# Attention in one fixed TensorE order over all 32 units, with 14 dense tiles woven in

## The chip, the cores and the metric

The kernel runs on one core of a Trainium2 chip. The metric is the device time of one execution in microseconds (us), the median of several runs. TensorE (PE; its weight loads are PEld) multiplies matrices and writes into PSUM, eight banks of 128 x 512 floats. VectorE (DVE), ScalarE (ACT) and GpSimd (POOL) work element by element; SyncE (SP) issues the transfers. Each engine has one queue of its own and works it in order; semaphores hold an instruction until what it needs is there.

## The reference

One layer of a streaming encoder: 1024 positions, width 1024. Attention picks 256 keys per query by an indexer's scores; beside it stands a Mamba-2 mixer (SSD); both are gated and merged; a SwiGLU follows. Cut to what the change touches:

```python
h = rmsnorm(x, pre_norm_mix) * (1.0 + scale_m) + shift_m
proj = h @ w_in          # columns: q_lat, kv_lat, k_idx, w_idx, z, xbc, dt, g_a, g_b
# A: attention, 16 heads of 128 latent columns, blocks of 128 queries
q = (rmsnorm(q_lat, q_norm) @ w_uq).reshape(B, L, 16, 128)
kv = rmsnorm(kv_lat, kv_norm)
_, idx = lax.top_k(iscore, 256)          # indexer scores, causal by chunks of 64
logits = einsum('bqhc,bqkc->bhqk', q_b, kv[idx]) * scale + rel_bias[bucket]
probs = softmax(where(valid, logits, -inf))
o = einsum('blhc,hcd->blhd', einsum('bhqk,bqkc->bqhc', probs, kv[idx]), w_uv)
# B: SSD
xbc = silu(causal_depthwise_conv(xbc, conv_w) + conv_b)   # 32 tiles of 128 channels
y = ssd(xbc, dt, a_log)
y = rmsnorm(y * silu(z), ssd_norm)                        # z: 16 tiles
mix = (sigmoid(g_a) * (o @ w_o_attn) + sigmoid(g_b) * (y @ w_o_ssd)) @ w_out   # g_a, g_b: 8 tiles each
```

## The kernel before, in words

Everything lies transposed: channels on the 128 partitions, positions along the row, in two halves of 512. Floats are split into a high and a low part, and a product is made of three (high x high, high x low, low x high). A dense tile of `w_in` (128 output channels, both halves) is therefore 48 TensorE products of 128 x 512; its sums stand in the tiles called `pw`. Weights come through a stream (`W`, lines 133 to 161): SP loads 128 x 512 floats, ScalarE copies the high part (line 151), GpSimd makes the low part (line 152), with three buffers of each.

Attention does not gather. Top-k (lines 616 to 716, VectorE and ScalarE) ends in a mask `MK` per block of queries (line 702); masked scores are computed for all keys. A **unit** is (hp, u): two heads, 256 queries (two blocks, t = 0 and 1), and so `2u + 2` blocks of 128 keys. There are 8 x 4 = 32 units, u in the order 0, 2, 1, 3. Each unit has two generators, which hand over control at every `yield`:

- `att_scores` (line 730): the query products `puq` (12 products), the copies `qh` on ScalarE (737) and `ql` on VectorE (738), and then, in four steps (t and head hh), the score products `plg` (766), VectorE's masked minimum out of PSUM (775) and ScalarE's Exp into `lg` (778).
- `att_out` (line 783): for each block j of keys a `turn`: two or four transposes of `lg` into a bank `pt` (799), and one copy `pc` out of it, on VectorE for odd j (802) and on ScalarE for even j (804). After all turns the products with the values `vt` (815), which use half of the array's columns and add up in the bank `po`, and the scaling and store (818 to 820).

`attention` (line 848) runs the scores of one unit beside the output of the unit before it through `weave`, which only sets the order of the program. The compiler's scheduler then orders each engine's queue anew, by a simulated timeline, with program order as priority: an instruction that is ready may pass one that is not. `in_order(...)` (line 108) ties the instructions of the named engines to program order; here `ATT_ORDER` is empty, so attention is not tied.

The order of the program is: indexer, top-k; attention of hp 0 to 2 (line 881); the dense tiles of `FILL` (line 936): five groups of four convolution tiles (`x`), 16 tiles of z, 8 of g_a, and three more convolution groups (`X`), 56 tiles in all; attention of hp 3 to 7 (line 947); SSD with the tiles of g_b and the attention projection beside it; merge; SwiGLU. A convolution tile ends in ScalarE's scaled copy (911), nine VectorE instructions (914 to 916) and Silu (921); for `X` two tiles share one chain of four Silu.

PSUM is split into two pools: three banks `bank_d` (dense tiles, and `pt` for hp 3 and above), five banks `bank` (`puq`, `plg`, `po`, and `pt` for hp below 3). `vt`, the values of two heads, has one buffer (855). After each unit `ada_next` (872) does a piece of the modulation vector (GpSimd, VectorE, two tiny products `adap`).

Of the kernel before, what the change touches and what calls it, by code (L numbers as in the profile page):

```python
# [17 lines left out]
P = 128  # L18
# [12 lines left out]
LOWEST = -BIGGEST  # L31
QC = 256
ORDERED = (mybir.EngineType.PE, mybir.EngineType.Activation, mybir.EngineType.DVE)
FILL = "xxxxx" + "z" * 16 + "a" * 8 + "XXX"
HP_FIRST = 3
LEAD = 1.5
U_ORDER = (0, 2, 1, 3)
ATT_ORDER = ()
NCH = L // QC
LAST = ((0, 0, 512), (1, 0, 256), (1, 256, 256))  # L40
FFN_GROUPS = [4, 4, 4, 4, 3, 3]
# [26 lines left out]
def build(tc, a, dbg=None, stop=99, slots=None):  # L68
# [26 lines left out]
    def half(b):  # L95
        return slice(512 * b, 512 * b + 512)
# [5 lines left out]
    def dump(key, ap, idx=None):  # L102
        if dbg is not None and key in dbg:
            d = dbg[key] if idx is None else dbg[key][idx]
            SP.dma_start(d, ap)
# [27 lines left out]
    class Stream:  # L133
# [21 lines left out]
        def next(self):  # L155
            self.used += 1
            while len(self.tiles) < min(self.used - 1 + self.ahead, len(self.q)):
                self.load()
            return self.tiles[self.used - 1]
# [11 lines left out]
    def col_tile(w):  # L171

        kt = w.shape[1]
        return [(w[:, k:k + min(4, kt - k)], min(4, kt - k)) for k in range(0, kt, 4)]
# [608 lines left out]
    def att_out(hp, u, vt, PR):  # L783

        r2 = sm.tile([P, 2, 2, 64], F32, name="r2", bufs=1)
        G.tensor_copy(r2, PR["rr"].rearrange("p (t h) -> p t h", t=2)[:, :, :, None].to_broadcast([P, 2, 2, 64]))
        po = bank("po")
        pov = po[:, 0:256].rearrange("p (t n) -> p t n", t=2)
        last = 2 * u + 1
        parts = {}  # L790

        def turn(j):
            ts = (0, 1) if j < last else (1,)
            sl = slice(ts[0], 2)
            pt = (bank if hp < HP_FIRST else bank_d)("pt")
            ptv = pt.rearrange("p (h t n) -> p h t n", h=2, t=2)
            for hh in range(2):
                for t in ts:
                    T.transpose(ptv[:, hh, t, :], PR[hh, t][:, j * P:(j + 1) * P], ident)  # L799
            pc = Q("pc").rearrange("p (h t n) -> p h t n", h=2, t=2)  # L800
            if j % 2:
                V.tensor_copy(pc[:, :, sl], ptv[:, :, sl])
            else:
                S.activation(pc[:, :, sl], ptv[:, :, sl], AF.Copy)
            parts[j] = pc, sl

        for j in range(last + 1):
            turn(j)
            yield
        for t in range(2):  # L810
            T.transpose(po[:, 256 + 128 * t:384 + 128 * t], r2[:, t].rearrange("p h n -> p (h n)"), ident)
        for j in range(last + 1):
            pc, sl = parts.pop(j)
            for hh in range(2):
                T.matmul(pov[64 * hh:64 * hh + 64, sl], vt[:, j, 64 * hh:64 * hh + 64], pc[:, hh, sl],
                         start=j == 0, stop=j == last, skip_group_check=True)
        rb = sm.tile([P, 256], F32, name="rb", bufs=1)
        S.activation(rb, po[:, 256:512], AF.Copy)
        V.tensor_tensor(rb, po[:, 0:256], rb, op=OP.mult)
        SP.dma_start(d_att[hp][:, 256 * u:256 * u + 256], rb)  # L820
        yield

    def weave(x, nx, y, ny, z=iter(()), nz=0, lead=1):

        i = j = k = 0
        while i < nx or j < ny:
            if j >= ny or (i < nx and i * ny <= j * nx * lead):
                next(x, None)
                i += 1
            else:  # L830
                next(y, None)
                j += 1
            while k < nz and k * (nx + ny) < nz * (i + j):
                next(z, None)
                k += 1
        for g in (x, y):
            for _ in g:
                pass
# [6 lines left out]

    att = {}

    def attention(steps, last, beside=lambda: None):

        for s_ in steps + [None] * last:  # L850
            nxt = iter(())
            if s_ is not None:
                hp, u = s_
                if u == U_ORDER[0]:
                    vt = vp.tile([P, NT, P], F32, name="vt", bufs=1)
                    SP.dma_start(vt, d_v[hp])
                    att["w"] = small_weights(a["w_uq"][hp]), vt, load_bias(hp)
                uq, vt, nb = att["w"]
                PR = {}
                nxt = att_scores(u, uq, nb, PR)  # L860
            prev = att.get("prev")
            if prev is None:
                weave(nxt, 5, iter(()), 0)
            else:
                weave(nxt, 5 if s_ else 0, att_out(*prev), 2 * prev[1] + 3, lead=LEAD)
            if s_ is not None:
                att["prev"] = (hp, u, vt, PR)
            beside()
# [3 lines left out]
    def ada_next():  # L872
# [3 lines left out]
            ada_col(*late.pop(0))  # L876
        if j is not None:
            late.append(ada_slow(j))

    if stop != 3:  # L880
        attention([(hp, u) for hp in range(HP_FIRST) for u in U_ORDER], 0, ada_next)
        if stop == 4:
            attention([(hp, u) for hp in range(HP_FIRST, 8) for u in U_ORDER], 1)
    if stop == 4:
        for k in range(KT):
            for b in BS:
                t = EV("attd")
                SP.dma_start(t, d_att[k][:, half(b)])
                dump("attn", t, (k, slice(None), half(b)))
        ctx.close()  # L890
        return


    def wide(c):
        W.plan(col_tile(a["w_in"][c]))
# [11 lines left out]
    def conv(ch, dst):  # L907
        p = wide(17 + ch)
        ts = [EV("cv") for b in BS]
        for b in BS:  # L910
            S.activation(ts[b], p[b], AF.Identity, bias=col("conv_b", ch), scale=col("cw3", ch))
        for s, nm_ in ((1, "cw2"), (2, "cw1"), (3, "cw0")):
            w = col(nm_, ch)
            V.scalar_tensor_tensor(ts[0][:, s:], p[0][:, :512 - s], w, ts[0][:, s:], op0=OP.mult, op1=OP.add)
            V.scalar_tensor_tensor(ts[1][:, :s], p[0][:, 512 - s:], w, ts[1][:, :s], op0=OP.mult, op1=OP.add)
            V.scalar_tensor_tensor(ts[1][:, s:], p[1][:, :512 - s], w, ts[1][:, s:], op0=OP.mult, op1=OP.add)
        return [(ts[b], dst[:, half(b)]) for b in BS]

    def conv_out(outs):
        for t, dst in outs:  # L920
            S.activation(t, t, AF.Silu)
            SP.dma_start(dst, t)

    def conv_group(g, n):

        tiles = ((16 + g, d_bc[g, 0]), (24 + g, d_bc[g, 1]), (2 * g, d_xs[2 * g]), (2 * g + 1, d_xs[2 * g + 1]))
        for i in range(0, 4, n):
            outs = [o for t in tiles[i:i + n] for o in conv(*t)]
            if n > 1:
                with in_order(mybir.EngineType.Activation):  # L930
                    conv_out(outs[::-1])
            else:
                conv_out(outs)

    n_x, n_z, n_a = iter(range(GROUPS)), iter(range(16)), iter(range(8))
    for kind in FILL:
        if kind in "xX":
            conv_group(next(n_x), 2 if kind == "X" else 1)
        elif kind == "z":
            t = next(n_z)  # L940
            gate(1 + t, d_z[t], AF.Silu)
        elif stop != 3:
            t = next(n_a)
            gate(49 + t, d_sga[t], AF.Copy)
    if stop != 3:
        with in_order(*ATT_ORDER):
            attention([(hp, u) for hp in range(HP_FIRST, 8) for u in U_ORDER], 1, ada_next)
    for _ in range(35):
        ada_next()

# [111 lines left out]
    def beside():  # L1062

        for t in range(8):
            W.plan(col_tile(a["w_in"][57 + t]))
            w = wpieces(ks8)
            for b in BS:
                p = bank_d("pw")
                yield from dense_steps(p, b, w, Hs)
                o = EV("g")  # L1070
                S.activation(o, p, AF.Copy)
                SP.dma_start(d_gb[t][:, half(b)], o)
                yield
        AT = [([None, None], [None, None]) for _ in range(KT)]
        for b in BS:
            for k in range(KT):
                t = EV("atl")
                SP.dma_start(t, d_att[k][:, half(b)])
                AT[k][0][b], AT[k][1][b] = split(H_, t, "at", lo_eng=G if k % 2 else V)
        for t in range(8):  # L1080
            W.plan(col_tile(a["w_o_attn"][t]))
            w = wpieces(ks8)
            for b in BS:
                ya = EV("ya")
                p = bank_d("poa")
                yield from dense_steps(p, b, w, AT)
                V.tensor_copy(ya, p)
                SP.dma_start(d_ya[t][:, half(b)], ya)
                yield
# [431 lines left out]
```

## Time and profile before

| | us |
|---|---|
| median of 3 runs | 2464.05 |
| the runs | 2463.94, 2464.05, 2467.35 |
| span of the profiled execution, first to last instruction | 2459.8 |
| median less span | 4.25 |
| TensorE busy in the span | 2383.1 |
| last attention output, its copy (line 819) | 1148.9 |

The profiled execution's own device time is not listed; its span is, and the 4.25 us lie around it. In the profile a row of a group gives line, engine, operation, output and inputs, shapes and count, then the busy time and the mean in ns, then the idle time of the engine ahead of them and what ended it. A matmul's row is longer than the time it keeps the array, because matmuls overlap: starts have to be compared, not lengths. A transpose is one record; a product of plain floats is two.

### The profile page before, as it was taken

What the parts mean: (1) busy time and instruction counts of PE and PEld (TensorE: products, weight loads), DVE (VectorE), ACT (ScalarE), POOL (GpSimd) and SP (SyncE); (2) the same over time, 40 slices, a digit from 0 to 9 for tenths busy, and PEclk for the clock granted to TensorE, in tenths of its full rate; (3) what the DMA queues carried; (4) which work ended last, traced back from release to release, by engine and by line L of the source; (5) the groups of instructions that cost most, each with busy time, mean ns of one, the idle gap of its engine ahead of it and who ended that gap; (6) DMA issues with size and microseconds to landing.
All of it is one profiled execution on the core that took longest, in us unless ns stands there. A gap on an engine that the chain in (4) does not pass through costs nothing. (4 is left out here: it accounts for less than half of the span.)

```text
span 2459.8 us, 34881 instructions
## 1 busy us (share of the span) xinstructions
PE 2383.1 (97%) x11946; PEld 1931.1 (79%) x11946; DVE 1496.3 (61%) x3050; ACT 1183.7 (48%) x2285; POOL 1022.3 (42%) x829
## 2 busy tenths in 40 slices
PE   7999999999999999999999999999999999999996
PEld 5788888888788887777776767888777888888886
DVE  4566775698745556765558666455476666552336
ACT  4446665567445545556566565544454222352211
POOL 2722112222234334553336335656676555432233
PEclk9999999999999999999999999999999999999998
DMA  7224122523212222223768775654465444253132
GB/s 268 99 77 130 65 73 78 155 87 103 86 67 92 102 99 91 93 84 123 223 215 260 228 246 172 231 186 161 168 208 171 160 145 163 99 190 113 48 99 90
DMA packets 212834, 341.25 MB, mean 139 GB/s; under 512 B 21249, under 2 KB 85425, under 8 KB 212657
## 3 DMA queue, kind: packets, MB, share of 16 engines
q1 hardware_dynamic: 211936, 338.45, 41.6%
q8 instruction: 94, 1.54, 0.3%
q14 instruction: 84, 0.68, 0.1%
q10 hardware_dynamic: 720, 0.58, 0.1%
HBM read 254.77 MB, written 87.32 MB: 139 GB/s over the span
## 5 line engine op out<-in xcount | busy, mean ns | idle before, releaser
L152 POOL TENSOR_TENSOR wlo<-wraw,whi 128x512 fp32r<-128x512 f32 (+1 forms) x282 | 380.7, 1351 | 769.4 <-ACT whi L151 698.5
L151 ACT ACTIVATE whi<-wraw 128x512 fp32r<-128x512 f32 (+1 forms) x282 | 175.4, 623 | 319.0 <-PE pfo L226 110.5
L1283 PE MATMUL p<-xh,wr 128*128 128x512 f32 x880 | 274.4, 391 | 3.8 <-DVE g L1333 3.6
L1283 PEld LDWEIGHTS p<-xh,wr 128*128 128x128 f32 x880 | 165.8, 188 | 39.1 <-DVE g L1333 4.0
L1277 POOL TENSOR_TENSOR wr<-a,wr 128x512 fp32r<-128x512 f32 x110 | 152.7, 1402 | 103.6 <-ACT wr L1276 70.6
L1283 PE MATMUL p<-xl,wr 128*128 128x512 f32 x440 | 171.8, 391 | 0.0
L778 ACT ACTIVATE lg<-lg,mx 128x256 f32<-128x256 f32 (+7 forms) x128 | 98.2, 769 | 74.7 <-DVE mx L775 73.5
L1276 ACT ACTIVATE wr<-a 128x512 fp32r<-128x512 f32 x110 | 67.7, 628 | 123.1 <-PE p L1283 98.0
L226 PE MATMUL pfo<-ah,wlo 128*128 128x512 f32 x304 | 118.1, 389 | 0.0
L226 PE MATMUL pfo<-al,whi 128*128 128x512 f32 x304 | 117.9, 389 | 0.0
L226 PE MATMUL pfo<-ah,whi 128*128 128x512 f32 x304 | 117.8, 389 | 0.0
L317 POOL TENSOR_TENSOR adaw<-adaw,cs 128x512 f32<-128x512 f32 x64 | 66.7, 1044 | 114.7 <-DMA adaw<-ada_w 109.4
L1398 DVE TENSOR_TENSOR facc<-facc,pfo 128x512 f32<-128x512 f32 x64 | 43.9, 686 | 112.0 <-PE pfo L226 112.0
L1283 PE MATMUL p<-h2h,wr 128*128 128x512 f32 x352 | 111.1, 393 | 0.0
L638 ACT ACTIVATE junk<-acc,cand__2203 128x1024 bf16<-128x1024 f32 (+2 forms) x96 | 86.2, 898 | 45.5 <-DVE cand__2203 L681 28.0
L226 PE MATMUL pos<-yw,whi 128*128 128x512 f32 x256 | 101.7, 397 | 3.6 <-DVE yw L1126 3.6
L226 PE MATMUL pos<-yh,whi 128*128 128x512 f32 x256 | 101.4, 396 | 1.7 <-ACT yh L1125 1.7
L226 PE MATMUL pos<-yh,wlo 128*128 128x512 f32 x256 | 101.5, 397 | 1.1 <-POOL wlo L152 1.1
L589 DVE SCALAR_TENSOR_TENSOR acc<-rel,widx,acc 128x384 f32<-128x384 f32 (+2 forms) x90 | 87.0, 986 | 24.9 <-ACT rel L584 24.7
L584 ACT ACTIVATE rel<-prel 128x512 f32<-128x512 f32 (+3 forms) x160 | 77.3, 524 | 48.4 <-PE prel L583 44.8
L1283 PEld LDWEIGHTS p<-xl,wr 128*128 128x128 f32 x440 | 83.0, 189 | 17.4
L799 PE MATMUL pt<-ident,lg 128*128 128x128 f32 x576 | 87.4, 277 | 7.1 <-ACT lg L778 6.6
(573 smaller groups left out, 6978.2 us busy)
## 6 DMA issues: line engine op xcount, KB each, us to landing
wraw<-w_in SPq DMA_DIRECT2D x130, 256.0 KB, 2.6
a<-w_ffn_in SPq DMA_DIRECT2D x124, 256.0 KB, 3.0
adaw<-ada_w SPq DMA_DIRECT2D x64, 256.0 KB, 2.7
al<-d_ac SPq DMA_DIRECT2D x32, 512.0 KB, 5.8
wraw<-w_o_ssd SPq DMA_DIRECT2D x64, 256.0 KB, 3.2
al<-d_a SPq DMA_DIRECT2D x44, 256.0 KB, 5.3
d_a<-g SPq DMA_DIRECT2D x40, 256.0 KB, 2.5
ada<-ada_p SPq DMA_DIRECT2D x16, 512.0 KB, 6.5
```

The costliest lines, as they stand in the source:

```text
L151: behind(S.activation(hi[:, :kt], raw[:, :kt], AF.Copy))
L152: behind(G.tensor_tensor(lo[:, :kt], raw[:, :kt], f(hi[:, :kt]), op=OP.subtract))
L226: T.matmul(o, wt[:, k0 + i, :], xs[k][xi][b][:, sl], start=pi == 0 and i == 0 and wt is hi and xi == 0, stop=pi == len(pcs) - 1 and i == l ...
L317: behind(G.tensor_tensor(t, t, cs[:, 4 * h:4 * h + 4, None].to_broadcast([P, 4, P]), op=OP.mult))
L584: S.activation(rel[:, 512 * b:512 * b + w_], pr[:, 0:w_], AF.Relu)
L589: V.scalar_tensor_tensor(acc[i][:, 0:n], rel[:, 0:n], ws, acc[i][:, 0:n], op0=OP.mult, op1=OP.add)
L638: S.activation(jk, y, AF.Sign, scale=-1.0, bias=a_, accum_out=o)
L778: S.activation(lg[:, 0:n], lg[:, 0:n], AF.Exp, scale=-1.0, bias=m, accum_out=mx[:, 3:4])
L799: T.transpose(ptv[:, hh, t, :], PR[hh, t][:, j * P:(j + 1) * P], ident)
L1276: S.activation(w[:, 0], src, AF.Copy)
L1277: G.tensor_tensor(w[:, 1], src, f(w[:, 0]), op=OP.subtract)
L1283: T.matmul(p, w[:, wi, i], X[x][i][xi], start=start and i == 0 and k == 0, stop=i == 3 and k == 2, skip_group_check=True)
```

## The change

All 32 units go into one call of `attention`, behind the dense tiles, and TensorE's order there is fixed to the order of the program. Of the 56 dense tiles 42 stay ahead of attention; 14 (two of g_a, three convolution groups) become a generator `woven`, whose tiles are cut into slices of six products. `attention` no longer uses `weave`: it writes the order of a step out by hand. The five pieces of the next unit's scores alternate with the turns of the unit before, which are dealt out in four portions; the last piece is the whole run of values' products; the slices are spread evenly over the pieces, eight in each of the first two steps and three in every later one. `pt` always comes from the three banks `bank_d`. A woven convolution tile finishes one half before it starts the other, and keeps the three last columns of the first half in `ends`.

```diff
-FILL = "xxxxx" + "z" * 16 + "a" * 8 + "XXX"
-HP_FIRST = 3
-LEAD = 1.5
+FILL = "xxxxx" + "z" * 16 + "a" * 6
+WOVEN = "aaXXX"
...
-            pt = (bank if hp < HP_FIRST else bank_d)("pt")
+            pt = bank_d("pt")
...
-    def attention(steps, last, beside=lambda: None):
-
-        for s_ in steps + [None] * last:
+    def attention(steps, beside, fill, nf):
+
+        for n, s_ in enumerate(steps + [None]):
...
-            if prev is None:
-                weave(nxt, 5, iter(()), 0)
-            else:
-                weave(nxt, 5 if s_ else 0, att_out(*prev), 2 * prev[1] + 3, lead=LEAD)
+            out, turns = (att_out(*prev), 2 * prev[1] + 2) if prev else (iter(()), 0)
+            order = [nxt]
+            for i in range(4):
+                order += [out] * (-(-(i + 1) * turns // 4) - order.count(out)) + [nxt]
+            order.append(out)
+            k = 0
+            for i, g in enumerate(order):
+                next(g, None)
+                while k < nf[n] and k * len(order) < nf[n] * (i + 1):
+                    next(fill, None)
+                    k += 1
...
-        attention([(hp, u) for hp in range(HP_FIRST) for u in U_ORDER], 0, ada_next)
...
+    def conv_steps(ch, dst, outs):
+
+        W.plan(col_tile(a["w_in"][17 + ch]))
+        w = wpieces(ks8)
+        ends = sm.tile([P, 3], F32, name="ends")
+        for b in BS:
+            p = bank_d("pw")
+            yield from dense_steps(p, b, w, Hs)
+            t = EV("cv")
+            S.activation(t, p, AF.Identity, bias=col("conv_b", ch), scale=col("cw3", ch))
+            if b == 0:
+                V.tensor_copy(ends, p[:, 509:512])
+            for s, nm_ in ((1, "cw2"), (2, "cw1"), (3, "cw0")):
+                c = col(nm_, ch)
+                V.scalar_tensor_tensor(t[:, s:], p[:, :512 - s], c, t[:, s:], op0=OP.mult, op1=OP.add)
+                if b:
+                    V.scalar_tensor_tensor(t[:, :s], ends[:, 3 - s:], c, t[:, :s], op0=OP.mult, op1=OP.add)
+            outs.append((t, dst[:, half(b)]))
+            yield
...
+    def woven():
+
+        for kind in WOVEN:
+            if kind == "a":
+                t = next(n_a)
+                yield from gate_steps(49 + t, d_sga[t])
             else:
-                conv_out(outs)
+                tiles = group_tiles(next(n_x))
+                for i in (0, 2):
+                    outs = []
+                    for t in tiles[i:i + 2]:
+                        yield from conv_steps(*t, outs)
+                    with in_order(mybir.EngineType.Activation):
+                        conv_out(outs[::-1])
...
-        with in_order(*ATT_ORDER):
-            attention([(hp, u) for hp in range(HP_FIRST, 8) for u in U_ORDER], 1, ada_next)
+    units = [(hp, u) for hp in range(8) for u in U_ORDER]
+    fill = woven()
+    with in_order(mybir.EngineType.PE):
+        attention(units, ada_next, fill, [8, 8] + [3] * 31)
+        for _ in fill:
+            pass
```

`gate_steps` is the same for a tile of g_a or g_b: six products, a `yield`, and after each half a ScalarE copy and the store.

More of the change, by code (lines that the diff above doesn't have):

```diff
@@ L33 @@
 ORDERED = (mybir.EngineType.PE, mybir.EngineType.Activation, mybir.EngineType.DVE)
-FILL = "xxxxx" + "z" * 16 + "a" * 8 + "XXX"
-HP_FIRST = 3
-LEAD = 1.5
+FILL = "xxxxx" + "z" * 16 + "a" * 6
+WOVEN = "aaXXX"
 U_ORDER = (0, 2, 1, 3)
-ATT_ORDER = ()
 NCH = L // QC
@@ L878, in ada_next @@
             late.append(ada_slow(j))
-    if stop != 3:
-        attention([(hp, u) for hp in range(HP_FIRST) for u in U_ORDER], 0, ada_next)
[L882 to L891, printed above, removed]
     def wide(c):
@@ L922, in conv_out, with group_tiles @@
             SP.dma_start(dst, t)
[L924 to L931, printed above, removed]
-            else:
-                conv_out(outs)
+    def group_tiles(g):
+        return (16 + g, d_bc[g, 0]), (24 + g, d_bc[g, 1]), (2 * g, d_xs[2 * g]), (2 * g + 1, d_xs[2 * g + 1])
@@ new lines, in conv_group @@
+    def conv_group(g):
+        for t in group_tiles(g):
+            conv_out(conv(*t))
+    def conv_steps(ch, dst, outs):
[16 more added lines that the diff above has]
+            yield
@@ new lines, in gate_steps @@
+    def gate_steps(c, dst):
+        W.plan(col_tile(a["w_in"][c]))
+        w = wpieces(ks8)
+        for b in BS:
+            p = bank_d("pw")
+            yield from dense_steps(p, b, w, Hs)
+            t = EV("g")
+            S.activation(t, p, AF.Copy)
+            SP.dma_start(dst[:, half(b)], t)
+            yield
+    def woven():
[3 more added lines that the diff above has]
+                yield from gate_steps(49 + t, d_sga[t])
+            else:
+                tiles = group_tiles(next(n_x))
[5 more added lines that the diff above has]
+                        conv_out(outs[::-1])
@@ L935, in build @@
     n_x, n_z, n_a = iter(range(GROUPS)), iter(range(16)), iter(range(8))
     for kind in FILL:
-        if kind in "xX":
-            conv_group(next(n_x), 2 if kind == "X" else 1)
+        if kind == "x":
+            conv_group(next(n_x))
         elif kind == "z":
@@ L941, in build @@
             gate(1 + t, d_z[t], AF.Silu)
-        elif stop != 3:
+        else:
             t = next(n_a)
             gate(49 + t, d_sga[t], AF.Copy)
-    if stop != 3:
-        with in_order(*ATT_ORDER):
-            attention([(hp, u) for hp in range(HP_FIRST, 8) for u in U_ORDER], 1, ada_next)
+    units = [(hp, u) for hp in range(8) for u in U_ORDER]
[4 more added lines that the diff above has]
+            pass
     for _ in range(35):
@@ L1064, in beside @@
         for t in range(8):
[L1065 to L1073, printed above, removed]
+            yield from gate_steps(57 + t, d_gb[t])
         AT = [([None, None], [None, None]) for _ in range(KT)]
```

## The prediction

> **What bounds the kernel now.** I read the page first, then the busy time of each engine in stretches, then TensorE's timeline around attention, and the waits last.
>
> ```profile
> span 2459.8 us, 34881 instructions
> PE 2383.1 (97%) x11946; PEld 1931.1 (79%) x11946; DVE 1496.3 (61%) x3050; ACT 1183.7 (48%) x2285; POOL 1022.3 (42%) x829
> ```
>
> ```profile
> 642.00:672.50 30.50, 24.41 (x109) 19.90 (x108) 30.36 (x40) 6.55 (x12) 7.62 (x4) 0.94 0.22 78
> 672.50:925.00 252.50, 252.50 (x1421) 207.19 (x1422) 139.11 (x437) 122.25 (x230) 97.51 (x92) 0.99 0.26 88
> 925.00:1149.00 224.00, 216.19 (x1515) 166.23 (x1514) 154.48 (x585) 123.52 (x276) 115.80 (x118) 1.00 0.30 97
> 1149.00:1460.00 311.00, 305.81 (x1652) 235.54 (x1651) 199.54 (x299) 185.65 (x411) 130.15 (x102) 0.99 0.70 223
> 1460.00:2459.00 999.00, 963.49 (x4332) 792.80 (x4331) 544.84 (x694) 372.20 (x652) 490.95 (x370) 0.98 0.46 153
> ```
>
> The columns are the stretch and its length, then the busy time of PE, PEld, DVE, ACT and POOL, the granted clock, and DMA. TensorE is the bound: 97% of the span, and 98% and 96% in the two stretches behind attention. So whatever TensorE saves before 1149 moves the end by as much. Attention runs from 672.5 to 1149 in two halves. Until 925, twelve units share TensorE with dense tiles and it never idles; from 925 twenty units run alone, idle 224.00 - 216.19 = 7.8 us, with VectorE at 154.48/224 = 69%. "Busy" hides a loss, though: what matters is how far apart matmuls start. The timeline shows it (start, length, engine, line, operation, count):
>
> ```profile
> 966.59 1.73 PE L815 MATMUL po<-pc,vt 128*64 128x256 f32 x16
> 968.25 0.38 PE L286 MATMUL adap<-ones,adas 128*128 128x1 f32 x2
> ...
> 979.32 0.28 PE L226 MATMUL puq<-qnh,uh 128*128 128x256 f32 x1
> 979.53 0.65 PE L815 MATMUL po<-pc,vt 128*64 128x256 f32 x4
> 980.11 0.38 PE L226 MATMUL puq<-qnl,uh 128*128 128x256 f32 x1
> 980.33 0.28 PE L226 MATMUL puq<-qnh,ul 128*128 128x256 f32 x1
> 980.45 0.28 PE L226 MATMUL puq<-qnh,uh 128*128 128x256 f32 x1
> ```
>
> Four records of the values' products (128*64: half the array's columns) take 0.58 us from start to start, sixteen take 1.66. The sixteen are twelve of 256 columns and four of 128 (their unit has four key blocks, the last half as wide), so 14 widths: one costs (1.66 - 0.58)/10 = 0.108. A puq product costs 980.45 - 980.33 = 0.12. From 979.32 to 980.33 pass 1.01 us for 0.12 + 4 x 0.108 + 0.12 = 0.67 of work: **entering and leaving such a run costs 0.34 us**, however long it is.
>
> ```profile
> 684.75 0.87 PE L815 MATMUL po<-pc,vt 128*64 128x256 f32 x8
> ...
> 1147.25 0.87 PE L815 MATMUL po<-pc,vt 128*64 128x256 f32 x8
> ```
>
> Between these first and last rows the timeline has 86 unbroken runs for 32 units: 23 until 925, 63 after. The scheduler, free to order TensorE, breaks the products of a unit into two or three pieces. The waits of the same stretch agree in kind:
>
> ```profile
> PEld po L815 <- issue: 13.3, 72, 0.5
> ...
> PE plg L766 <- DVE mx L775: 4.3, 5, 1.0
> ...
> PE pt L799 <- ACT pc L804: 0.5, 1, 0.5
> ```
>
> 72 times the weight load of these products sat idle with no semaphore to wait for (0.185 us each; the part of the price seen on the load side).
>
> **The change part by part.** *Products in one run.* In the new program the order of TensorE is the program's from the first unit to the last, and a unit's products are its last piece, after all its transposes: 32 runs for 86. 54 x 0.34 = 18.4 us less, all on the bound. Ends: 54 x 0.185 = 10 and 54 x 0.35 = 19; I take 18.4, the row that holds both sides of the switch.
>
> *Work moved ahead.* The list of dense tiles before attention goes from 56 to 42 tiles of 48 products; 14 are woven in.
>
> ```profile
> 0.00:672.50 672.50, 486.77 (x2041) 380.53 (x2041) 92.66 (x180) 56.48 (x84) 0.99 0.33 112
> 672.50:925.00 252.50, 155.78 (x627) 114.95 (x628) 50.88 (x100) 20.01 (x27) 0.99 0.26 88
> ```
>
> (Instructions that touch the tile pw.) Before 672.5 TensorE had done 2041 of these products; the new list has 42 x 48 = 2016, so nearly the same work lies ahead, and the 14 tiles replace the same 13.5 in attention. No TensorE work is added. What can vanish is the hole ahead of the first transposes:
>
> ```profile
> 665.77 0.39 PE L226 MATMUL pw<-h3h,wlo 128*128 128x512 f32 x1
> 666.00 0.39 PE L226 MATMUL pw<-h4h,whi 128*128 128x512 f32 x1
> 672.48 0.47 PE L799 MATMUL pt<-ident,lg 128*128 128x128 f32 x1 [6.09 <-ACT lg L778]
> ...
> 673.07 0.52 PE L766 MATMUL plg<-kvtl,qh 128*128 128x384 f32 x1
> 673.39 0.52 PE L766 MATMUL plg<-kvth,ql 128*128 128x384 f32 x1
> ...
> 675.85 0.33 PE L766 MATMUL plg<-kvth,ql 128*128 128x384 f32 x1
> 676.02 0.28 PE L766 MATMUL plg<-kvth,qh 128*128 128x256 f32 x1
> ```
>
> 6.1 us idle, and then half speed (0.32 us between rows that later take 0.17) from 672.5 to about 675.8, which loses half of 3.3: 1.7 us more. The first two units of the new order carry 8 slices each, 16 x 6 = 96 products x 0.23 = 22 us, which need no mask. But the hole has another cause as well:
>
> ```profile
> 671.93 0.40 ACT L778 ACTIVATE lg<-lg,mx 128x128 f32<-128x128 f32 x1 [8.93 <-DVE mx L775]
> ```
>
> ```profile
> 675.41 0.43 DVE L702 TENSOR_SCALAR mk<-run 128x512 bf16<-128x512 f32 x1
> ```
>
> ScalarE stood 8.93 us at the first Exp, behind VectorE's last mask work, and the copies of weights and of finished tiles that feed slices are queued behind it on the same engine. If the new order of ScalarE does the same, the slices starve too. Between 0 and 7.8 us I take 4.
>
> *Old idle time out, new idle time in.* The 7.8 us after 925 belong to an order that is gone. The fixed order waits at its head whenever an operand is late, and two kinds of lateness can be priced. (a) Ordinary latency: a unit's scores wait for its query (puq, then copies on ScalarE and VectorE), transposes wait for Exp, banks wait for copies.
>
> ```profile
> L804 ACT ACTIVATE pc<-pt 128x512 f32<-128x512 f32 x80 | 46.0, 595 | 54.9 <-PE pt L799 53.9 <-POOL nm L750 0.7
> ...
> L802 DVE COPY pc<-pt 128x512 f32<-128x512 f32 x48 | 32.9, 685 | 13.7 <-PE pt L799 13.2
> ...
> L738 DVE SCALAR_TENSOR_TENSOR ql<-puq,qh 128x512 fp32r<-128x512 f32 x30 | 20.7, 690 | 36.9 <-ACT qh L737 36.8
> ...
> L737 ACT ACTIVATE qh<-puq 128x512 fp32r<-128x512 f32 x30 | 17.6, 588 | 25.0 <-PE puq L226 25.0
> ```
>
> The query needs 0.59 + 0.69 = 1.3 us; in the new order a slice of 6 x 0.23 = 1.4 us stands right behind puq, so it is just covered when neither engine is behind. Uncovered, the stretch after 925 lost (7.8 - 2.1)/20 = 0.29 us a unit (the 2.1 belong to the next item); 32 units would lose 9; 4.3 us of the 7.8 were scores that waited for VectorE to empty a bank. With cover the stretch before 925 lost 0. I take 5. VectorE gets no fuller on average: 139.11 + 154.48 = 294 us over some 457, 64%.
>
> (b) Silu. Each pair of woven convolution tiles ends in four Silu, and Exp and Silu each load their table:
>
> ```profile
> 935.99 1.28 ACT L921 ACT_TABLE_LOAD   x1 [3.07 <-DVE mod L287]
> 937.28 2.19 ACT L921 ACTIVATE cv<-cv 128x512 f32<-128x512 f32 x4
> ...
> 939.64 0.58 ACT L737 ACTIVATE qh<-puq 128x512 fp32r<-128x512 f32 x1
> ...
> 940.73 1.28 ACT L778 ACT_TABLE_LOAD   x1
> ```
>
> ```profile
> 940.28 0.44 PE L766 MATMUL plg<-kvth,qh 128*128 128x384 f32 x1 [2.06 <-ACT qh L737]
> ```
>
> ```profile
> L921 ACT ACT_TABLE_LOAD x6 | 7.7, 1283 | 15.7 <-DVE cv L916 11.6 <-DVE mod L287 4.0
> ```
>
> Before and after there are six such blocks. From 935.99 to 942.01 ScalarE is closed to Exp, 6.0 us. Five blocks cost TensorE nothing, since dense tiles filled in; the last, with no tile left, cost 2.06. In the fixed order the tiles cannot come forward. Ends 0 and 6 x 6.0 = 36; I take 1 us each, between the five free ones and the one paid, because three slices a unit still stand in between: 6. The row speaks of 1.28 us per load, and the next instruction starts at its end. The Trainium skill, ScalarE: Activation LUTs, section What ACT_TABLE_LOAD costs, would add a drain of about 1.38 us to each switch, 2.66 in all; by it each block would be 2.8 us longer and this estimate, spread alike, about 9 instead of 6. The trace shows no such drain.
>
> Free by cover: the copy of three columns that the convolution's second half now reads (12 small VectorE instructions at 64% load); the loads of vt, whose single buffer is now released at the very end of a step, a whole step before the next use; SP issues nothing new. If the vt load were late, the last piece of eight steps would wait.
>
> **Sum:** 18.4 + 4 + 7.8 - 5 - 6 = 19.2 us. Span 2459.8 - 19.2 = 2440.6; the median of the runs lies 4.25 above the profiled span, so 2464.05 - 19.2 = 2444.9, **2445 us**. A difference under 0.2% (4.9 us) cannot be told from none.
>
> **Rivals.** *A: Silu blocks decide, slower.* Everything TensorE is to gain, 18.4 + 4 + 7.8 - 5 = 25.2, is spread over six blocks: above 4.2 us each the change loses. With TensorE pinned and ScalarE closed 6.0 us, 36 us are lost: 2464.05 + 10.8 = 2474.9. For it: the 2.06 was paid exactly where no dense tile stood by, and the block begins with ScalarE standing still (3.07). Against: transposes, products and slices that need nothing of ScalarE lie within a unit. Chance 0.09. By the page's drain the blocks would be 8.8 us and the time 2492.
>
> *B: banks, no change.* Transposes and dense tiles now share three PSUM banks for all units. One bank accumulates a tile; the order issues 48 pairs of consecutive transposed blocks, and if a bank is still being emptied the second block waits for one copy, (0.595 + 0.685)/2 = 0.64 us. Half the pairs: 15 us, time 2460; all pairs: 31 us, 2476. For it: VectorE peaks near 69% already. Against: the units after 925 used the same three banks for transposes with one wait of 0.5 us in all on a copy (pt on pc above). Chance 0.13. The Trainium skill, TensorEngine Tiling (Array Packing), section PSUM Bottleneck, warns that tiling speeds TensorE and not the emptying of PSUM; this rival is that rule, and the rows after 925 do not show it yet.
>
> *C: the products gain nothing.* The 0.34 could be a wait for the copied block, which one run would pay too. Then 2464.05 - 0.8 = 2463. Against: runs of 4 and of 16 carry the same surcharge, and no copy is named as releaser. Chance 0.04.
>
> *D: the order covers everything.* No new idle time and the whole hole gone: 18.4 + 7.8 + 7.8 = 34, time 2430. For it: the stretch with tiles idled 0. Chance 0.14.
>
> **How the numbers follow.** The forecast, 2438 to 2455, has the remaining 0.60. The range 2428 to 2466 takes in D and C and most of B and leaves out A and B's far end, some 0.13. Faster by over 0.2% (under 2459.1): forecast, D and part of B, 0.81. Within 0.2%: the rest of B and C, 0.10. Slower: A, 0.09.
>
> **What would show it.** Right: 32 runs of L815, each of 8 to 32 records, the issue idle of their weight load down by more than half; TensorE busy through 666 to 676 or a hole under 4 us; the last copy of attention near 1129; the stages behind it unchanged in length. Wrong: holes of TensorE of 3 us or more behind a Silu table load (A); waits of pt on pc, dozens of them (B); 0.34 us still lost per piece although the pieces are one (C).

## The result, and the profile after

The changed kernel takes 2483.01 us, the median of four runs (2478.41 to 2486.38), beside 2463.99 us (four runs) for the kernel before: the ratio is 1.0075, 95% interval 1.006 to 1.0089. It is slower by some 19 us, where 19 us less were forecast. The profiled execution took 2478.41 us, the shortest of the four. First its page, span and TensorE's busy time, to be set beside the page of before (2459.8 and 2383.1):

```profile
span 2476.6 us, 34836 instructions
PE 2377.0 (96%) x11946; PEld 1936.5 (78%) x11946; DVE 1505.9 (61%) x3062; ACT 1189.5 (48%) x2285; POOL 1021.9 (41%) x829
```

TensorE does the same number of instructions and is busy 6.1 us less, but it stands idle 2476.6 - 2377.0 = 99.6 us where it was 76.7. The busy time by stretches says where (columns as in the prediction: stretch, length, PE, PEld, DVE, ACT, POOL, granted clock, DMA):

```profile
642.00:676.00 34.00, 22.65 (x102) 18.85 (x101) 33.07 (x42) 6.45 (x11) 8.84 (x6) 0.86 0.20 62
676.00:925.00 249.00, 238.90 (x1523) 195.73 (x1522) 149.82 (x516) 122.41 (x252) 106.75 (x106) 1.00 0.26 80
925.00:1156.60 231.60, 217.51 (x1402) 176.36 (x1401) 147.83 (x500) 121.79 (x245) 102.57 (x101) 1.00 0.30 95
1156.60:1470.00 313.40, 308.78 (x1669) 239.52 (x1669) 198.45 (x306) 191.36 (x420) 131.85 (x103) 0.99 0.71 225
```

Ahead of attention 34.00 - 22.65 = 11.4 us are idle (before: 6.1), and then 10.1 until 925, where nothing was lost before, and 14.1 from 925 to the last product with the values (before: 7.8). So 35.5 us stand idle from 642 to the end of attention. The fewer pieces are there too. The groups of the values' products, before and after (busy us, mean ns, idle ahead), and the idle time of their weight load after (before: 13.3 us, 72 times):

```profile
L815 PE MATMUL po<-pc,vt 128*64 128x256 f32 (+1 forms) x640 | 81.2, 371 | 0.3 <-DMA vt<-d_v 0.3
```

```profile
L813 PE MATMUL po<-pc,vt 128*64 128x256 f32 (+1 forms) x640 | 69.3, 363 | 0.0
```

```profile
PEld po L813 <- issue: 5.4, 32, 0.2
```

32 runs came in place of 86, and 32 such waits in place of 72. The weight load is idle 7.9 us less and the products' own rows are 11.9 us shorter. These two must not be added: the weight load works beside the products, and the end of a row overlaps the next. TensorE as a whole is busy only 6.1 us less.

**The start.** TensorE, VectorE and ScalarE around the end of the masks (start, length, engine, line, operation, and in brackets the idle time ahead and what ended it):

```profile
661.80 0.28 PE L764 MATMUL plg<-kvth,qh 128*128 128x256 f32 x1
661.92 0.28 PE L764 MATMUL plg<-kvtl,qh 128*128 128x256 f32 x1
673.55 0.58 PE L764 MATMUL plg<-kvth,ql 128*128 128x256 f32 x1 [11.35 <-DVE ql L736]
```

```profile
672.15 0.74 DVE L698 SCALAR_TENSOR_TENSOR run<-run,tm__2217,eq 128x512 f32<-128x512 f32 x1
672.82 0.68 DVE L736 SCALAR_TENSOR_TENSOR ql<-puq,qh 128x512 fp32r<-128x512 f32 x1
```

```profile
674.74 0.40 ACT L776 ACTIVATE lg<-lg,mx 128x128 f32<-128x128 f32 x1 [13.59 <-DVE mx L773]
```

The first unit's query is ready for `ql` at 659.9, but in VectorE's queue `ql` stands behind the mask work of line 698 and starts at 672.82. TensorE has its third score product next in its fixed order and stands for 11.35 us; the slices behind it need no mask, but in a fixed order they cannot pass. ScalarE stands 13.59.

**Inside attention.** Waits of TensorE from 685 to 1160 (what waits, for whom: us in all, times, longest), and those of VectorE for GpSimd's sum of bias and mask `nm` in attention, after and before:

```profile
PE plg L764 <- DVE mx L773: 11.1, 10, 1.8
PE pt L797 <- DVE pc L800: 4.6, 8, 1.6
PE pt L797 <- DVE cv L936: 4.3, 8, 1.3
PE pt L797 <- ACT pc L802: 3.5, 5, 1.1
```

```profile
DVE lg L773 <- POOL nm L748: 68.4, 34, 4.6
```

```profile
DVE lg L775 <- POOL nm L750: 14.0, 11, 3.4
```

TensorE waits for banks that VectorE and ScalarE have not emptied, and VectorE itself waits five times as long as before, 34 times, for GpSimd. One case, on GpSimd, VectorE and TensorE:

```profile
745.19 0.40 POOL L784 COPY r<-rr 128x256 f32<-128x256 f32 x1 [2.17 <-DVE rr L777]
751.55 1.04 POOL L315 TENSOR_TENSOR adaw<-adaw,cs 128x512 f32<-128x512 f32 x1 [5.96 <-DMA adaw<-ada_w]
752.55 1.16 POOL L748 TENSOR_TENSOR nm<-nb,mk 128x512 f32<-128x512 f32 x1
```

```profile
753.74 0.42 DVE L773 CUSTOM_DVE_ANT_0 lg<-plg,nm 128x256 f32<-128x256 f32 x1 [4.39 <-POOL nm L748]
```

```profile
754.94 0.35 PE L764 MATMUL plg<-kvth,qh 128*128 128x256 f32 x1 [1.11 <-DVE mx L773]
```

`nm` needs only the bias and the mask, which have long been there. But in GpSimd's queue it stands behind `r`, the copy of the last unit's reciprocals, which waits for the last Exp, and behind `adaw`, which waits 5.96 us for a transfer. VectorE takes the first score 4.39 us late, its bank comes free late, TensorE waits.

### The profile page after: what moved, and what is told of

It is laid out like the page before. It is cut to its first block, busy times and chain, and to the rows that moved or that the text cites. A ratio compares the mean times of both kernels' runs of the same rounds, so it can differ in the third digit from the quotient of the medians.

```text
span 2476.6 us, 34836 instructions
## 1 busy us (share of the span) xinstructions
PE 2377.0 (96%) x11946; PEld 1936.5 (78%) x11946; DVE 1505.9 (61%) x3062; ACT 1189.5 (48%) x2285; POOL 1021.9 (41%) x829
## 5 line engine op out<-in xcount | busy, mean ns | idle before, releaser
L773 DVE CUSTOM_DVE_ANT_0 lg<-plg,nm 128x256 f32<-128x256 f32 (+1 forms) x128 | 50.8, 403 | 82.0 <-POOL nm L748 68.4
```

## The experiments

Two causes were proposed: H, the late start at the masks, and W, waits at the head of the fixed order that come from the other engines' queues. (The expectation of run 1 uses W for something else, the weaving and the shared banks.) Rivals, where the texts name them by letters: P, that the fixed order as such costs; the prediction's A (Silu), B (banks) and C (the products gained nothing). Kernel 2 is the kernel of experiment 2, and so on.

All ratios are to runs of the kernel before on the same chip. A ratio's interval is some 0.14% to either side (3.4 us), so a difference of two kernels is good to 5 us. Beside it stands the mark, the start of the last product with the values in the profiled execution: 1147.8 before, 1156.2 after. Marks and spans come from one execution each, and that one can lie away from the median of its kernel: 4.6 us below it for the changed kernel and 7.1 below for run 5, 7.2 above for run 1, 5.6 above for run 8 and 4.2 above for run 9.

**1. The order not fixed.**

```diff
-    with in_order(mybir.EngineType.PE):
+    with in_order():
```

> The changed kernel with nothing tied to program order in attention: the weaving, the 14 tiles in slices and the three shared banks stay, only TensorE's fixed order goes. The scheduler now cuts the values' products into 106 runs. Theory P (the fixed order costs: it waits at its head): the hole ahead of the masks shrinks from 11 us to about 6, the waits of TensorE in attention from 24 us to under 10, and 20 runs more than before cost 20 x 0.34 = 7 us: 2468 to 2474. Rival W (the weaving and the shared banks cost, whatever the order): 2478 or more, with transposes still waiting for copies.

Measured: 2490.81 us, ratio 1.010 [1.0086, 1.0115], last product at 1178.9; 106 runs.

```profile
PEld po L813 <- issue: 16.2, 83, 0.4
```

```profile
PE plg L764 <- ACT qh L735: 6.6, 3, 3.0
PE pt L797 <- ACT lg L776: 4.2, 5, 2.4
...
PE plg L764 <- DVE mx L773: 0.3, 1, 0.3
```

The waits for the banks all but go (the scores' 11.1 on VectorE becomes 0.3, the transposes' 12.4 become 1.4), so it is the fixed order that turns lateness into waits. But the products fall apart into more pieces than before, and the time rises. P falls: this program is no better in a free order. Nor does the late start come from the fixed order alone, since in a free order it still costs 8.1 us:

```profile
PE plg L764 <- DVE ql L736: 8.1, 1, 8.1
```

**2. The first unit's scores ahead of the dense tiles**, outside the fixed order; then 12 slices, then the steps in the fixed order, four slices in the first and three in every later one.

```diff
+    attention(units[:1], ada_next, iter(()), [0], 0)
     for kind in FILL:
...
-        attention(units, ada_next, fill, [8, 8] + [3] * 31)
+        for _ in range(12):
+            next(fill)
+        attention(units[1:], ada_next, fill, [4] + [3] * 31)
```

> The changed kernel with the scores of the first unit put ahead of the dense tiles, outside the fixed order, and 12 of the first 16 slices ahead of the first transposes. Theory H (the hole of 11.35 us is the first unit's ql, queued on VectorE behind all the mask work while TensorE is tied to wait for it): ql is done 200 us earlier, the hole falls to 5 us or less and the time by 6 to 10 us, to 2473 to 2477. Rival S (ScalarE standing at the first Exp starves the slices of weights and of their copies): the hole stays near 11 us under another name, time 2480 to 2485.

Measured: 2470.49 us, ratio 1.0020 [1.0006, 1.0033]; last product 1149.6, 6.6 earlier. The hole is now 2.07 + 1.27, behind weights:

```profile
675.98 0.50 PE L234 MATMUL pw<-h4h,whi 128*128 128x512 f32 x1 [2.07 <-ACT whi L149]
...
677.98 0.66 PE L234 MATMUL pw<-h4h,wlo 128*128 128x512 f32 x1 [1.27 <-POOL wlo L150]
```

H holds; the 12 to 14 us by the medians and ratios are more than the 6 to 10 expected, the mark's 6.6 and the spans' 9.7 (2476.6 to 2466.9) are not. The waits inside attention are unchanged (scores on VectorE 10.1 us, 9 times).

**3. All copies out of the transposes' banks on ScalarE**, to take work off VectorE (1505.9 us busy in the changed kernel, 1465.0 here).

> The changed kernel with all copies of transposes (pc) on ScalarE instead of every second one on VectorE, some 46 us of work moved. Theory Q (VectorE's queue is what makes banks late: transposes wait behind convolution work, scores behind both): the 8.9 us of waits of pt on VectorE and most of the 11.1 us of plg on VectorE go, with as much again that hides inside the matmul rows; waits on ScalarE grow by a few us: 2465 to 2474. Rival N (three banks are too few whichever engine empties them, or ScalarE becomes the late one): the waits of pt only change their name and the time stays within 4 us of 2483 or rises.

Measured: 2481.61 us, ratio 1.0069 [1.0056, 1.0083]; last product 1156.5, 0.3 later.

```profile
PE pt L797 <- ACT pc L799: 11.3, 13, 1.4
PE po L810 <- ACT pc L799: 7.3, 4, 2.2
PE plg L764 <- DVE mx L773: 6.2, 6, 1.1
```

A miss for the theory, as the rival expected: the waits changed names and stayed. How much VectorE has to do was not it.

**4. The products of a unit cut in two** (63 runs), the next unit's last piece between.

```diff
+            if j == u:
+                yield
...
-            order.append(out)
+            order[-1:] = [out, nxt, out]
```

> The changed kernel with the values' products of each unit cut into two runs, with the last piece of the next unit's scores between them: 63 runs instead of 32, nothing else added. Theory: a run costs 0.34 us to enter and leave, so 31 x 0.34 = 10.5 us more, 2491 to 2496. Rival C (no price of entering; the 0.34 was waiting for copies): within 3 us of 2483.

Measured: 2495.93 us, ratio 1.0127 [1.0111, 1.0142]: 0.0052 above the changed kernel, 12.8 us for 31 runs, 0.41 each, 0.25 to 0.57 by the interval; last product 1177.3, 21.1 later. Not all of that is the runs': transposes now also wait 6.8 us for Exp, which they did not before. In the profiled execution TensorE is busy 12.1 us more (2389.1), 0.39 a run, and idle 5.6 us more. Rival C, by which a piece more costs nothing, falls.

**5. One run in the kernel before**, nothing else of the change: a tie of order, without a semaphore, holds a unit's products until its last two copies (43 runs; the cut leaves out the lines that collect `copies`).

```diff
+                for name in copies[-2:] if j == 0 else ():
+                    tc.add_manual_dep(i.ins, name, mybir.DependencyInfo(
+                        mybir.DependencyClass.NoSync, mybir.DependencyReason.DATA), reason="one run")
```

> One part of the change alone: the kernel before, with the values' products of a unit held back only until the unit's last two copies have been made, so that they come in 43 runs instead of 86; order, dense tiles and everything else as before. The theory of the price (a run of products costs what it lost in the kernel before, 0.34 us, or the 0.41 us that 31 more runs cost when the fixed order's run was cut in two) expects 43 x 0.34 to 0.41 = 15 to 18 us less than before, about 2449 us. The rival, that holding the products back only moves the loss into later waits (fewer short products between the copies, the transposes' banks late), expects a gain under 6 us and new waits of the transposes on their copies.

Measured: 2454.33 us, ratio 0.9956 [0.9939, 0.9972], 10.8 us less than before, where 15 to 18 were expected: 0.25 us a run, 0.15 to 0.35 by the interval. In the profiled execution, the shortest of six, TensorE's busy time is 2383.1 - 2368.1 = 15.0 us less and its idle time about the same (77.3):

```profile
PE 2368.1 (97%) x11946; PEld 1934.3 (79%) x11946; DVE 1491.7 (61%) x3050; ACT 1183.6 (48%) x2285; POOL 1021.2 (42%) x829
```

Half of these 15.0 us lie behind attention: from 20 us after the last product to the end TensorE is busy 1242.7 us for 5863 products, before 1250.1 for 5878, and 15 products are some 3.5 us. So about 4 us of the 15.0 are not the runs', and 0.25 is the better price.

**6. The sums `nm` a step ahead**, on kernel 2: both sums of a unit are traced in the middle of the step before, ahead of `r` (the cut leaves out the helpers that make them).

```diff
+                if i == len(order) // 2 and s_ is not None and s_ != units[-1]:
+                    att["nm"] = masks_of(*units[units.index(s_) + 1])
```

> On the kernel with the first unit's scores ahead of the dense tiles (2470 us), GpSimd's two sums of bias and mask of a unit are made in the middle of the step before it, ahead of the copy of the reciprocals in GpSimd's queue, instead of behind it. The theory that VectorE's waits for these sums (64.3 us, 34 times) are what makes the score banks and the copies late for the fixed order expects these waits to fall under 20 us, TensorE's waits in the stretch (10.1 on the maximum, 4.1 and 3.6 on the copies, 5.1 on the convolution) to fall by half, and with what hides in the rows 10 to 15 us less: about 2457 us. The rival, that VectorE's wait lay beside slack and TensorE waits for VectorE's own work, expects VectorE's wait to fall and the time to stay within 4 us of 2470.

Measured: 2457.51 us, ratio 0.9968 [0.9958, 0.9979]; last product 1133.5, 16.1 earlier. VectorE waits no more for `nm` (no such row is left), and of TensorE's waits on VectorE's maximum none is left either. The longest of TensorE's waits that remain in attention:

```profile
PE pt L805 <- ACT lg L784: 3.5, 5, 1.1
PE pt L805 <- ACT pc L810: 3.0, 5, 0.7
PE pt L805 <- DVE cv L951: 1.7, 4, 0.4
```

Busy time of the stretch from 685 to 1158, kernel 2 and this one:

```profile
685.00:1158.00 473.00, 448.82 (x2878) 365.67 (x2877) 298.96 (x1016) 241.29 (x488) 207.57 (x205) 1.00 0.28 89
```

```profile
685.00:1158.00 473.00, 462.15 (x2967) 377.79 (x2966) 311.99 (x1028) 256.31 (x514) 210.55 (x208) 1.00 0.29 93
```

24.2 us idle become 10.9. W holds, with GpSimd's queue as its source.

**7. Silu left out** on kernel 2 (a plain copy in the twelve woven tiles).

> On the kernel with the first unit's scores ahead (2470 us), the Silu of the twelve woven convolution tiles is a plain copy, so ScalarE loads no other table inside attention; the Silu itself is left out there. The prediction's rival A (blocks of Silu with their table loads hold ScalarE's queue, and TensorE with it) expects 6 to 30 us less. The theory that the waits at the head of the order come from VectorE's and GpSimd's queues expects under 4 us less, and the same waits of TensorE on the maximum and the copies.

Measured: 2464.55 us, ratio 0.9996 [0.9987, 1.0005]: 5.9 us less than kernel 2, at the border of the two expectations; last product 1144.4, 5.2 earlier. The waits on VectorE's maximum are the same:

```profile
PE plg L764 <- DVE mx L773: 9.6, 10, 1.2
```

**8. Kernel 5 with the sums a step ahead** (free order, 38 runs).

> The kernel before, in its free order, with the values' products held back to one run (38 runs) and the two sums of bias and mask of a unit made a step ahead. If VectorE's waits for these sums cost time in every order, they cost here in the measure of their size in the trace (12.8 us of such waits with the products held back, against 64.3 us that were worth 13 us in the fixed order): about 3 us, and five runs fewer about 1.5 us more, so about 2450 us. If they matter only where the order is fixed, because a free order lets TensorE's instructions be placed around them, the time stays within 2 us of 2454 us, but for the runs.

Measured: 2445.32 us, ratio 0.9919 [0.9906, 0.9931]. By the ratios 9 us less than kernel 5, more than either expectation; by the last product (1141.0 to 1137.6) 3.4. The sums, with five runs fewer, count in the free order too, but by how much stays open. Of the kernels that leave nothing out it has the lowest ratio, 20 us below before; kernel 10 lies within the interval.

**9. The changed kernel with the sums a step ahead**, alone.

> The changed kernel with the sums of bias and mask a step ahead and nothing else; the first unit's scores still stand behind the dense tiles. If the two causes (the late start at the masks, 12.5 us by the other experiment, and the sums behind the reciprocals, 13 us) are separate and add up, it is 2483 - 13 = 2470 us with the hole at the start still there. If the waits in attention were echoes of the late start, the gain is under 5 us, 2478 us or more.

Measured: 2460.04 us, ratio 0.9981 [0.9971, 0.9991]: 23 us less than the changed kernel by the ratios, where 13 were expected; last product 1140.0, 16.2 earlier. The hole at the start is still there:

```profile
PE plg L772 <- DVE ql L746: 11.4, 5, 10.0
```

By the marks the causes add up: 6.6 (H) and 16.2 (`nm`) for 22.7 together; by the spans too, 9.7 and 14.2 for 24.1. By the ratios they don't: 13.6 and 23 for 26. This discord of 10 us is more than the 6 us that the intervals of the four kernels allow together, and it stays open. So both causes are shown, but the size of `nm` is known only as 13 to 23 us.

**10. Every second turn in the scores' banks**, on kernel 6.

```diff
-            pt = bank_d("pt")
+            pt = (bank_d, bank)[j % 2]("pt")
```

> On the kernel with both repairs (2457 us), every second turn of the transposes takes its bank from the five that the scores use, and no longer from the three that it shares with the dense tiles. The prediction's rival B (three banks shared by the transposes and the dense slices make a pair of transposed blocks wait for a copy) expects the waits of the transposes on their copies and on the convolution (3.0, 1.2 and 1.7 us) to go and 5 to 10 us less than 2457. The theory that these waits are only where the lateness of VectorE and ScalarE shows expects the waits to move to the scores' banks and the time within 4 us of 2457, on either side.

Measured: 2447.85 us, ratio 0.9936 [0.9921, 0.995]; last product 1129.7. By the ratios 8 us less than kernel 6, by the mark 3.8. The waits for the copies and the convolution are gone, and those that are left are for data:

```profile
PE pt L805 <- ACT lg L784: 3.8, 7, 0.7
PE pw L234 <- POOL wlo L150: 3.1, 1, 3.1
```

**11. The same edit alone in the changed kernel.**

> The changed kernel with one edit: every second turn of the transposes takes its bank from the scores' five. If the three shared banks are a cause of their own, they are worth here what they were worth in the repaired kernel, about 10 us: 2473 us. If they only pass on the lateness of VectorE and ScalarE, the waits move: the scores, which already wait 11.1 us for a bank, wait longer with turns in their banks, and the time stays within 4 us of 2483 or rises. Whichever way, the waits of the transposes for the convolution (4.3 us) and for the copies (8.1 us) should fall by half.

Measured: 2475.35 us, ratio 1.0041 [1.0027, 1.0055]: 8 us less, last product 1152.0, 4.2 earlier. The transposes' waits for copies and convolution go entirely; the scores' stay, and others come:

```profile
PE plg L764 <- DVE mx L773: 10.8, 8, 1.7
PE plg L764 <- DVE ql L736: 8.1, 7, 2.4
PE pt L797 <- ACT lg L776: 2.5, 4, 1.1
```

So the three shared banks are a cause of their own, 4 to 8 us.

**12. Silu left out with all three repairs** (kernel 10, a plain copy in the woven tiles).

> The kernel with all three repairs (first unit's scores ahead, sums a step ahead, every second turn in the scores' banks; 2448 us), with the Silu of the twelve woven tiles a plain copy; the Silu itself is left out there. If the blocks of Silu cost the fixed order time of their own, as the 6 us between 2470 and 2464 us say, they do so here: about 2442 us. If they cost only where the other queues are late already, the time stays within 3 us of 2448.

Measured: 2442.19 us, ratio 0.9911 [0.9894, 0.9929]: 6 us less than kernel 10 by the ratios, 9.1 by the mark (1120.6). Together with run 7: Silu costs the fixed order some 6 us, each of the two good to 4 or 5.

## Why the prediction was wrong

Two steps failed outright, both in the idle time that the new order brings: the hole at the masks, and the ordinary latency. A third came short: the saving was not there in full. The measured 2483 us also lie beyond what rivals A (2474.9) and B (2476 at its far end) give by the rows.

**The balance of TensorE**, by the profiled executions. The span was to fall by 19.2 us and rose by 16.8, 36.0 off. The busy time was to fall by 18.4 and fell by 6.1: 12.3 off. The idle time was to fall by 0.8 (4 and 7.8 out, 5 and 6 in) and rose by 22.9: 23.7 off.

**Products in one run: the count right, the saving short.** 32 runs came. The price of 0.34 us lies between 0.25 (run 5) and 0.41 (run 4), and inside both intervals. But 54 runs fewer should then have taken 14 to 22 us off the busy time, and 6.1 went. The kept traces narrow this down. Take attention's own products (queries, scores, transposes, values, `adap`) and add up the time from each record's start to the next one's, without the idle time shown. That makes 331.6 us before, 322.7 after, 320.0 in run 5, 332.0 in run 4 and 316.4 in run 10. By this count a run costs 0.27 us (run 5) or 0.30 (run 4). The changed kernel saves only 8.9 us for its 54 runs, and with the three repairs 15.2 for 53. What lies between may be waits too short to open a gap between rows; that is argued, not shown.

**Work moved ahead: wrong, 7 to 14 us.** I took 4 us as gained, because 96 products of slices need no mask. I followed ScalarE's queue, but not the query: in the program before the first unit was traced ahead of all dense tiles, and its `ql` lay far from the masks. Moved behind them, `ql` stands in VectorE's queue behind the last mask work, and TensorE's fixed order has the product that needs it ahead of the slices. The hole grew to 11.35 us. Run 2 puts the unit back and is worth 6.6 us by the mark, 9.7 by the spans (2476.6 to 2466.9) and 13.6 by the ratios.

**Old idle time out, new idle time in, (a) ordinary latency: wrong; this is the step that decided.** I took 5 us, from what the free order had lost per unit. A free order hides lateness by running something else, so its waits are no measure of how late the operands are: in run 1 the same program, not tied, shows 0.3 us of the scores' 11.1. The row to read was VectorE's wait for `nm`, 14.0 us before, 68.4 after, and behind it GpSimd's queue, which I had not looked at. The sums ahead of `r` and `adaw` are worth 14 us by the spans (2476.6 to 2462.4; 2466.9 to 2452.5), 16 by the marks, 13 to 23 by the ratios. Which of the two, `r` or `adaw`, holds them more was not separated.

**(b) Silu: right in size.** 6 us were taken, 6 measured (runs 7 and 12, each good to 4 or 5). The 1 us a block was chosen between 0 and 6.0, so that it fits so well is in part luck. A block in the changed kernel, on ScalarE:

```profile
859.59 1.28 ACT L912 ACT_TABLE_LOAD   x1
860.89 2.19 ACT L912 ACTIVATE cv<-cv 128x512 f32<-128x512 f32 x4
863.09 1.28 ACT L776 ACT_TABLE_LOAD   x1
864.39 0.51 ACT L776 ACTIVATE lg<-lg,mx 128x256 f32<-128x256 f32 x1
```

Each load ends where the next instruction starts, within 0.02 us; the drain that the Trainium skill (ScalarE: Activation LUTs, What ACT_TABLE_LOAD costs) adds to a switch does not appear here either. Rival A did not decide: leaving Silu out is worth 6 us of the 36.

**B, banks: in part.** Half the pairs were priced at 15 us; the edit is worth 8 us by the ratios (runs 10 and 11), 4 by the mark. The rows of before showed 0.5 us of such waits, since a free order goes around a full bank: in run 1 the transposes wait 1.4 us for banks, in the fixed order 12.4. The rule of the Trainium skill that the prediction weighed (TensorEngine Tiling (Array Packing), PSUM Bottleneck), that tiling speeds up TensorE and not the emptying of PSUM, fits this, but no run here changes the tiling.

**The stages behind: not unchanged.** From the last product to the end pass 1320.4 us after and 1312.0 before. TensorE's busy time from 20 us after the last product on, before and after:

```profile
1168.20:2459.80 1291.60, 1250.10 (x5878) 1014.02 (x5876) 737.42 (x981) 544.47 (x1033) 615.57 (x467) 0.98 0.52 170
```

```profile
1176.60:2476.60 1300.00, 1258.52 (x5918) 1021.92 (x5916) 739.96 (x989) 552.21 (x1050) 620.54 (x470) 0.98 0.53 170
```

40 more instructions and 8.4 us more work are left: the free order had drawn that much of the next stage into attention. This is work in another place, not time lost. It is missing ahead of the mark, and behind it TensorE is idle 41.5 us in both.

By the spans the three repairs, one after the other, are worth 9.7 (the late start), 14.4 (the sums) and 5.5 (the banks, 2452.5 to 2447.0), 29.6 of the 36.0 us. They cannot simply be added to the forecast, which held 5 us for latency and gained 4 at the hole. Kernel 10 stays 6.4 us above the forecast's span of 2440.6 (its median of 2447.85 us is 2.9 above the forecast's 2444.9), and what these 6.4 us are was not separated. That the repaired kernel comes so near the forecast does not bear the forecast out: one repair also takes out the `nm` waits that were there before the change.

## What to carry to other kernels

Before an engine's order is fixed, look up for each operand at its head which engine makes it and what stands ahead of that instruction in that engine's queue, with its own waits; the time an operand needs when all is idle (here 1.3 us for the query) says little. Waits in a freely ordered trace can be far below those of a fixed order, since the free order went around the rest: 14.0 us became 68.4 here. And a good part of such a change may be had alone: holding the products back in the free order and making the sums a step earlier gave 20 us, the whole change lost 19.

## What the runs showed that was not expected

Moving two instructions of 1.16 us in each unit on GpSimd, an engine 41% busy, was worth 13 us or more on TensorE, 96% busy, two engines away.

And the busy time of a group can mislead. The third product of each score, `kvth,ql`, seems to have grown from 58.2 to 66.6 us (188 and 192 of them in the stretch):

```profile
L766 PE MATMUL plg<-kvth,ql 128*128 128x384 f32 (+2 forms) x188 | 58.2, 352 | 0.0
```

```profile
L764 PE MATMUL plg<-kvth,ql 128*128 128x512 f32 (+2 forms) x192 | 66.6, 347 | 11.9 <-DVE ql L736 11.8
```

But one of them is no longer than before, 347 ns in the mean against 352. A group's busy time counts overlap once. Before, the free order often put two or three of them side by side; after, each stands alone, and 192 x 347 ns are the 66.6 us. The first row is of before, the second of after:

```profile
1002.79 0.80 PE L766 MATMUL plg<-kvth,ql 128*128 128x512 f32 x3
```

```profile
753.43 0.40 PE L764 MATMUL plg<-kvth,ql 128*128 128x512 f32 x1
```

So these rows show no loss. The products' own rows (81.2 and 69.3 us) say as little by themselves, since fewer runs also mean fewer overlapping ends. Only starts, or the busy time of the whole engine, can be compared.
